# Layer norm of eight token tiles: five of them moved from ScalarE and GpSimd to VectorE

## The chip, the cores and the metric

The kernel runs on one core of a Trainium2 chip. The metric is the device time of one execution in microseconds (us). The core has five engines that run side by side: TensorE (PE in the rows; its weight loads are PEld), VectorE (DVE), ScalarE (ACT), GpSimd (POOL) and SyncE (SP), which here issues all the DMAs. Each engine works through its own instructions in order and waits on semaphores of the others.

## The reference

A decoder trunk of two layers over a stream x of 1024 tokens by 1024 channels, in float32. In each layer a projection of x feeds four token mixers; their gated outputs are merged, projected by `w_out`, and the stream is renewed by a layer norm, which is all that this change touches:

```python
def _layer_norm(x, g, b):
    mu = jnp.mean(xf, axis=-1, keepdims=True)
    var = jnp.mean(jnp.square(xf - mu), axis=-1, keepdims=True)
    y = (xf - mu) * lax.rsqrt(var + LN_EPS)
    return y * g + b
...
    out = merged @ w_out
    return _layer_norm(DEEPNORM_ALPHA * x + out, ln_g, ln_b)
```

## The kernel before

Tokens are cut into eight tiles of 128 (the partitions); a row of 1024 channels is two halves of 512. At the end of a layer the output projection runs in two passes, `col` 0 and then `col` 1, each over tiles t = 0 to 7. For one tile TensorE does 24 matmuls (8 blocks of k, three float32 products each, L245 to L247) into a PSUM tile `po`. VectorE then forms `res = ALPHA * xr + po` (L1218, `xr` is the old stream, loaded from DRAM) and its statistics (L1219). In the pass `col` 1 the row is complete, and `ln(t)` (L1160) follows at once: mean and variance (L1163, L1165), two small ScalarE activations that make a first rsqrt (L125, tiles `rs_t` and `rstd`), and one Newton step on VectorE (L1176 to L1178).

What follows depends on the tile. For t of 5, 6 and 7 (`direct`) VectorE does all of it: (res - mean) * gain for both halves (L1175) ahead of the Newton step, and (that) * rstd + bias for both halves behind it (L1181). For t of 0 to 4 VectorE makes -mean * rstd (L1184), ScalarE normalizes each half (L1186), GpSimd multiplies by the gain (L1187) and adds the bias (L1188). Gain and bias (`lnp`) are loaded once for each layer (L1208). The result `xo` is stored half by half by SyncE: to `xs` in layer 0, to `out` in layer 1.

Layer 0 goes straight over into layer 1. While the `po` matmuls of tiles 5 to 7 run, TensorE transposes tiles 0 to 3 of `xo` (`xtp`, L206); ScalarE copies each transposed block out of PSUM and rounds it (`xTr`, `xTh`, L210, L211), and GpSimd takes the remainder (`xTl`, L212). The weights `wA` of layer 1's first projection are loaded (L568), split by ScalarE (`wAh`, L576) and GpSimd (`wAl`, L577). Then `pA` begins, the first matmuls of layer 1: tokens of tiles 0 to 3 at first; the transposes of tiles 4 to 7 are placed among them. Layer 1's norm is the end of the program.

The order on every engine is set at build time by a scheduler that works from the program's order and its own cost model. Most [128, 512] tiles share a pool of 64 buffers (`U`), and [128, 1024] ones a pool of 7 (`W`).

Of the kernel before, what the change touches and what calls it, by code (L numbers as in the profile page):

```python
# [13 lines left out]
AF = mybir.ActivationFunctionType  # L14
ALU = mybir.AluOpType
# [4 lines left out]
P = 128  # L20
# [45 lines left out]
def decoder_trunk(ctx: ExitStack, tc: tile.TileContext, x, x_t, mem_t, positions, w_a, w_s, mla_q_norm, mla_w_qb,  # L66
                  mla_kv_norm, mla_w_kvb, fox_forget_bias, w_out,
                  ln_gain, ln_bias, out, dump=None):
    nc = tc.nc
    act, dve, pool, pe = nc.scalar, nc.vector, nc.gpsimd, nc.tensor  # L70
# [19 lines left out]
    def U(s, dt=F32R):  # L90
        return up.tile([P, HALF], dt, tag="U", name=nm(s))

    def W(s, w=S):
        if w <= HALF:
            return U(s, F32)[:, :w]
        return wp.tile([P, S], F32, tag="W", name=nm(s))[:, :w]
# [4 lines left out]
    def SM(s, n=1):  # L101
        return sp.tile([P, 16], F32, tag="sm", name=nm(s))[:, :n]
# [21 lines left out]
    def tfn(*args, **kw):  # L124
        i = act.activation(*args, **kw)  # L125
        if table_load[0] is not None:
            after(i, table_load[0])
        table_users.append(i)
# [501 lines left out]
    for layer in range(DEPTH):  # L630
# [252 lines left out]
        for b in range(0, NB, 2):  # L883
            t = U("ckv", F32).rearrange("p (b c) -> p b c", b=2)
# [269 lines left out]
        gb = []  # L1154
        res = {}
        nat = {}
        cs = [slice(0, HALF), slice(HALF, D)]
        dst = out[0] if last_layer else xs

        def ln(t):  # L1160
            direct = t >= 5
            mv = SM("mv", 2)
            dve.bn_aggr(mv, stats[:, t])  # L1163
            m, r, u = SM("var", 1), SM("rstd", 1), SM("rs_t", 1)
            dve.tensor_scalar(m, mv[:, 1:2], 1e-5, 1.0, ALU.add, ALU.mult)  # L1165
            tfn(u, m, AF.Ln)
            tfn(r, u, AF.Exp, scale=-0.5)
            if t < 5:
                o = W("xo")
                os = [o[:, c] for c in cs]  # L1170
            else:
                os = [U("xo", F32), U("xo", F32)]
            if direct:
                for half, c in enumerate(cs):
                    dve.scalar_tensor_tensor(os[half], res.pop((t, half)), mv[:, 0:1], gb[0][:, c], ALU.subtract, ALU.mult)  # L1175
            dve.scalar_tensor_tensor(u, r, m, r, ALU.mult, ALU.mult)  # L1176
            dve.tensor_scalar(u, u, -0.5, 1.5, ALU.mult, ALU.add)
            dve.tensor_tensor(r, r, u, ALU.mult)  # L1178
            if direct:
                for half, c in enumerate(cs):  # L1180
                    dve.scalar_tensor_tensor(os[half], os[half], r, gb[1][:, c], ALU.mult, ALU.add)  # L1181
                    nc.sync.dma_start(dst[t * P:(t + 1) * P, c], os[half])
            else:
                dve.scalar_tensor_tensor(mv[:, 1:2], mv[:, 0:1], -1.0, r, ALU.mult, ALU.mult)  # L1184
                for half, c in enumerate(cs):
                    act.activation(os[half], res.pop((t, half)), AF.Identity, scale=r, bias=mv[:, 1:2])  # L1186
                    pool.tensor_tensor(os[half], os[half], gb[0][:, c], ALU.mult)  # L1187
                    pool.tensor_tensor(os[half], os[half], gb[1][:, c], ALU.add)  # L1188
                    nc.sync.dma_start(dst[t * P:(t + 1) * P, c], os[half])
            nat[t] = [os[k // 4][:, (k % 4) * P:(k % 4) * P + P] for k in range(KT)]  # L1190

        xrs = []
# [11 lines left out]
        for col in range(2):  # L1204
            if col:
                for src in (ln_gain, ln_bias):
                    g = W("lnp")
                    nc.sync.dma_start(g, src[layer].partition_broadcast(P))  # L1208
                    gb.append(g)
            for t in range(NB):  # L1210
                fetch(4)
                if not col:
                    wo[1].append(wload_o(w_out[layer], t, 1, "wo", "U"))
                ps = PJ("po")
                toks = [tuple(m[:, (t % 4) * P:(t % 4) * P + P] for m in merged[(k, t // 4)]) for k in range(KT)]
                drain(weave(passes(ps, toks, wo[col], KT), early_x, 2, t == NB - 1))
                r = U("res", F32)
                dve.scalar_tensor_tensor(r, xrs.pop(0), ALPHA, ps, ALU.mult, ALU.add)  # L1218
                dve.bn_stats(stats[:, t, col], r)  # L1219
                res[(t, col)] = r  # L1220
                if col:
                    ln(t)
                    if t == 4 and not last_layer:
                        early_x = transpose_x(0, [nat.pop(i) for i in range(4)], True)
                    if t == 5 and not last_layer:
                        load_wA(layer + 1, 0, 4)
                        split_wA()
            wo[col] = None
# [64 lines left out]
```

## Time and profile before

| | us |
|---|---|
| median of 3 runs | 1590.06 |
| lowest and highest of them | 1589.1 and 1591.06 |
| profiled execution | 1590.93 |
| its span, first to last instruction | 1589.2 |
| busy: TensorE, VectorE, GpSimd, ScalarE | 1559.1, 1035.0, 834.8, 739.9 |

The profile is of one execution. Times in the rows count from the start of its span; 1.73 us of its time lie around the span. "Busy" is the sum of an engine's instructions. A row of a timeline that covers several like instructions (x2) gives the stretch that they take together.

### The profile page before, as it was taken

Reading aid. Unit: us, or ns where it says so; the run is one execution under the profiler, and the core shown is the slowest. Engines: PE = TensorE matmul, PEld = TensorE weight load, DVE = VectorE, ACT = ScalarE, POOL = GpSimd, SP = SyncE. Lnnn points to the kernel's source line nnn. Section 1 sums busy time; section 2 is a strip of 40 time slices with the busy share of each in tenths; the row PEclk is TensorE's granted clock in tenths of the full one; section 3 lists DMA queues with packets and bytes.
Section 4 is the critical chain, followed back from the end, with each engine's and each line's share of the span. In section 5 each row is a group of like instructions: output and inputs, shape, how many; then the busy total and the mean of one; then the engine's idle time right before and its main releaser. Section 6 shows DMA issues by size and latency. Waiting matters only on the chain.

```text
span 1589.2 us, 24849 instructions
## 1 busy us (share of the span) xinstructions
PE 1559.1 (98%) x8454; PEld 1332.1 (84%) x8454; DVE 1035.0 (65%) x2025; ACT 739.9 (47%) x1632; POOL 834.8 (53%) x991
## 2 busy tenths in 40 slices
PE   9999999999999999999999999999999999999997
PEld 8888888888888888888788888888888878888885
DVE  7456689844436788872763566898444367888638
ACT  4355656534424656440423556555344346564302
POOL 5676435765544344671836655267655433446515
PEclk9999999999999999999999999999999999999999
DMA  6311112142233211252312221122422332212413
GB/s 183 114 57 55 48 39 64 54 127 61 79 102 110 68 58 40 82 177 73 116 61 87 60 61 44 37 64 64 116 61 84 100 104 70 64 49 75 146 53 113
DMA packets 86062, 127.93 MB, mean 80 GB/s; under 512 B 13424, under 2 KB 38832, under 8 KB 85936
## 3 DMA queue, kind: packets, MB, share of 16 engines
q1 hardware_dynamic: 85936, 126.34, 25.6%
q8 instruction: 67, 1.10, 0.3%
q14 instruction: 59, 0.48, 0.1%
HBM read 89.57 MB, written 19.96 MB: 69 GB/s over the span
## 4 chain that ended last, share of the span: by engine, by line
PE 85%; DVE 7%; issue 2%; DMA 2%; POOL 2%; ACT 1%; SPq 0%; DVEq 0%; ACTq 0%; POOLq 0%
PE pj L245 12%; PE pj L246 12%; PE pj L247 12%; PE y L485 7%; PE pt L455 6%; PE sc L366 3%; PE sc L367 3%; PE pb L245 3%; PE po L245 3%; PE po L247 3%; PE po L246 3%; PE pb L247 3%; PE pb L246 3%; PE pg L245 2%; PE pg L247 1%
## 5 line engine op out<-in xcount | busy, mean ns | idle before, releaser
L245 PE MATMUL pj<-xTh,wh 128*128 128x512 f32 x832 | 331.6, 399 | 2.2 <-DVE mx L424 1.4
L247 PE MATMUL pj<-xTh,wl 128*128 128x512 f32 x832 | 326.5, 392 | 0.0
L246 PE MATMUL pj<-xTl,wh 128*128 128x512 f32 x832 | 326.0, 392 | 0.0
L157 POOL TENSOR_TENSOR wl<-wr,wh 128x512 fp32r<-128x512 f32 x168 | 229.9, 1370 | 9.8
L154 POOL TENSOR_SCALAR wh<-wr 128x512 fp32r<-128x512 f32 x168 | 116.3, 692 | 209.7 <-PE pj L246 112.9
L146 DVE TENSOR_TENSOR pl<-pt,ph 128x384 fp32r<-128x384 f32 (+1 forms) x272 | 170.4, 638 | 75.3 <-ACT ph L145 73.4
L145 ACT CAST ph<-pt 128x384 fp32r<-128x384 f32 (+1 forms) x272 | 147.0, 550 | 133.9 <-PE pt L455 127.6
L247 PEld LDWEIGHTS pj<-xTh,wl 128*128 128x128 f32 x832 | 156.4, 188 | 31.8
L245 PEld LDWEIGHTS pj<-xTh,wh 128*128 128x128 f32 x832 | 156.8, 188 | 28.8 <-DVE mx L424 1.8
L246 PEld LDWEIGHTS pj<-xTl,wh 128*128 128x128 f32 x832 | 156.8, 189 | 25.4
L436 POOL TENSOR_SCALAR p<-p,sm 128x896 f32<-128x896 f32 (+7 forms) x128 | 102.4, 801 | 144.0 <-DVE sm L435 142.4
L125 ACT ACTIVATE p<-p,mx 128x896 f32<-128x896 f32 (+7 forms) x128 | 99.5, 778 | 70.7 <-DVE mx L424 63.2
L485 PE MATMUL y<-pl,v 128*128 128x256 f32 (+1 forms) x544 | 125.5, 307 | 0.0
L125 ACT ACTIVATE mg<-pg 128x512 f32<-128x512 f32 x128 | 76.4, 597 | 88.0 <-PE pg L247 58.9
L485 PE MATMUL y<-ph,v 128*128 128x256 f32 (+1 forms) x544 | 112.6, 284 | 0.1
L455 PE MATMUL pt<-ident_r,p 128*128 128x128 f32 x704 | 110.5, 272 | 0.0
L245 PE MATMUL pb<-ybh,wh 128*128 128x512 f32 x256 | 102.9, 402 | 2.2 <-DVE opB L295 1.0
L485 PEld LDWEIGHTS y<-ph,v 128*128 128x128 f32 x544 | 93.7, 190 | 12.3 <-issue 0.9
L429 DVE TENSOR_TENSOR_SCAN kt<-kt,unseen 128x896 f32<-128x896 f32 (+3 forms) x64 | 94.5, 1489 | 10.1 <-ACT kt L125 9.8
L246 PE MATMUL pb<-ybl,wh 128*128 128x512 f32 x256 | 100.1, 391 | 0.0
L247 PE MATMUL pb<-ybh,wl 128*128 128x512 f32 x256 | 100.1, 391 | 0.0
L416 POOL TENSOR_SCALAR_AFFINE_SELECT bt<-bt 128x128 f32<-128x128 f32 x64 | 47.5, 745 | 95.0 <-ACT bt L125 91.2
(277 smaller groups left out, 3658.0 us busy)
## 6 DMA issues: line engine op xcount, KB each, us to landing
wr<-in_w_s_dram SPq DMA_DIRECT2D x168, 256.0 KB, 2.6
s<-opA SPq DMA_DIRECT2D x128, 64.0 KB, 2.0
s<-opB SPq DMA_DIRECT2D x128, 64.0 KB, 2.0
wr<-in_w_out_dram SPq DMA_DIRECT2D x32, 256.0 KB, 2.6
xr<-in_x_t_dram SPq DMA_DIRECT2D x16, 256.0 KB, 5.1
ckb<-c_d SPq DMA_DIRECT2D x8, 512.0 KB, 3.8
y_d<-y SPq DMA_DIRECT2D x16, 256.0 KB, 2.0
y<-y_d SPq DMA_DIRECT2D x16, 256.0 KB, 3.6
```

The costliest lines, as they stand in the source:

```text
L125: i = act.activation(*args, **kw)
L145: act.copy(h, src)
L146: return dve.tensor_tensor(l, src, f(h), ALU.subtract)
L154: i = pool.tensor_scalar(h, src, 1.0, 1.0, ALU.mult, ALU.mult)
L157: pool.tensor_tensor(l, src, f(h), ALU.subtract)
L245: pe.matmul(ps, ah, bh, start=k == 0, stop=False)
L246: pe.matmul(ps, ah, bl, start=False, stop=False)
L247: pe.matmul(ps, al, bh, start=False, stop=k == nk - 1)
L429: dve.tensor_tensor_scan(kt[:, ::-1], kt[:, ::-1], unseen[:, S - w:][:, ::-1], 1.0, ALU.mult, ALU.max)
L436: pool.tensor_scalar(p, p, sm, 1.0, ALU.mult, ALU.mult)
L455: pe.transpose(pt[:, c:c + P], self.p[i][:, b * P:(b + 1) * P], ident)
L485: pe.matmul(u.y[:, q0 * P:256], u.op["v"][b][:, u.head, :], src[:, s * 256 + q0 * P:s * 256 + 256], start=j == 0 and n == 0, stop=j == n_c ...
```

## The change

All eight tiles now take the path that tiles 5 to 7 took: the branch on `direct` and the one for ScalarE and GpSimd are gone, and nothing else is altered. The buffers stay as they were: a `W` tile for t of 0 to 4, two `U` tiles for the rest.

```diff
--- before.py
+++ after.py
@@ -1158,7 +1158,6 @@
         dst = out[0] if last_layer else xs
 
         def ln(t):
-            direct = t >= 5
             mv = SM("mv", 2)
             dve.bn_aggr(mv, stats[:, t])
             m, r, u = SM("var", 1), SM("rstd", 1), SM("rs_t", 1)
@@ -1170,23 +1169,14 @@
                 os = [o[:, c] for c in cs]
             else:
                 os = [U("xo", F32), U("xo", F32)]
-            if direct:
-                for half, c in enumerate(cs):
-                    dve.scalar_tensor_tensor(os[half], res.pop((t, half)), mv[:, 0:1], gb[0][:, c], ALU.subtract, ALU.mult)
+            for half, c in enumerate(cs):
+                dve.scalar_tensor_tensor(os[half], res.pop((t, half)), mv[:, 0:1], gb[0][:, c], ALU.subtract, ALU.mult)
             dve.scalar_tensor_tensor(u, r, m, r, ALU.mult, ALU.mult)
             dve.tensor_scalar(u, u, -0.5, 1.5, ALU.mult, ALU.add)
             dve.tensor_tensor(r, r, u, ALU.mult)
-            if direct:
-                for half, c in enumerate(cs):
-                    dve.scalar_tensor_tensor(os[half], os[half], r, gb[1][:, c], ALU.mult, ALU.add)
-                    nc.sync.dma_start(dst[t * P:(t + 1) * P, c], os[half])
-            else:
-                dve.scalar_tensor_tensor(mv[:, 1:2], mv[:, 0:1], -1.0, r, ALU.mult, ALU.mult)
-                for half, c in enumerate(cs):
-                    act.activation(os[half], res.pop((t, half)), AF.Identity, scale=r, bias=mv[:, 1:2])
-                    pool.tensor_tensor(os[half], os[half], gb[0][:, c], ALU.mult)
-                    pool.tensor_tensor(os[half], os[half], gb[1][:, c], ALU.add)
-                    nc.sync.dma_start(dst[t * P:(t + 1) * P, c], os[half])
+            for half, c in enumerate(cs):
+                dve.scalar_tensor_tensor(os[half], os[half], r, gb[1][:, c], ALU.mult, ALU.add)
+                nc.sync.dma_start(dst[t * P:(t + 1) * P, c], os[half])
             nat[t] = [os[k // 4][:, (k % 4) * P:(k % 4) * P + P] for k in range(KT)]
 
         xrs = []
```

The scheduler's orders change at the end of each layer alone. On ScalarE and GpSimd the five tiles' instructions drop out (10 activations and 20 tensor_tensor in each layer), and the others keep their order. Below, `mv` is mean and variance, `var`, `rs_t` and `rstd` are [128, 1] tiles, and lines behind L1160 have other numbers after the change (L1173 was L1175, L1178 was L1181, L1208 was L1218).

VectorE, layer 0, tile 0, before:

```order
L1163 BN_AGGR mv_8673<-bst_8344 128x2
L1165 TENSOR_SCALAR var_8675<-mv_8673 128x1
L1176 SCALAR_TENSOR_TENSOR rs_t_8677<-rstd_8676,var_8675 128x1
L1177 TENSOR_SCALAR rs_t_8677<-rs_t_8677 128x1
L1178 TENSOR_TENSOR rstd_8676<-rstd_8676,rs_t_8677 128x1
L1184 SCALAR_TENSOR_TENSOR mv_8673<-mv_8673,rstd_8676 128x1
L1218 SCALAR_TENSOR_TENSOR res_8721<-xr_8567,po_8696 128x512
```

and after:

```order
L1162 BN_AGGR mv_8673<-bst_8344 128x2
L1164 TENSOR_SCALAR var_8675<-mv_8673 128x1
L1173 SCALAR_TENSOR_TENSOR xo_8681<-res_8384,mv_8673,lnp_8639 128x512
L1173 SCALAR_TENSOR_TENSOR xo_8681<-res_8670,mv_8673,lnp_8639 128x512
L1174 SCALAR_TENSOR_TENSOR rs_t_8677<-rstd_8676,var_8675 128x1
L1175 TENSOR_SCALAR rs_t_8677<-rs_t_8677 128x1
L1176 TENSOR_TENSOR rstd_8676<-rstd_8676,rs_t_8677 128x1
L1178 SCALAR_TENSOR_TENSOR xo_8681<-xo_8681,rstd_8676,lnp_8641 128x512 x2
L1208 SCALAR_TENSOR_TENSOR res_8718<-xr_8567,po_8693 128x512
L1209 BN_STATS bst_8344<-res_8718 128x6
```

The two gain instructions stand between the variance and the Newton step, so that they run while ScalarE makes `rstd`; the two bias instructions stand ahead of the next tile's `res`.

VectorE, layer 0, tiles 6 (`mv_9070`) and 7 (`mv_9117`), after the change; before it the order there is the same:

```order
L1173 SCALAR_TENSOR_TENSOR xo_9078<-res_8600,mv_9070,lnp_8639 128x512
L1173 SCALAR_TENSOR_TENSOR xo_9079<-res_9067,mv_9070,lnp_8639 128x512
L1208 SCALAR_TENSOR_TENSOR res_9114<-xr_8835,po_9089 128x512
L1174 SCALAR_TENSOR_TENSOR rs_t_9074<-rstd_9073,var_9072 128x1
L1209 BN_STATS bst_8344<-res_9114 128x6
L1175 TENSOR_SCALAR rs_t_9074<-rs_t_9074 128x1
L1162 BN_AGGR mv_9117<-bst_8344 128x2
L1176 TENSOR_TENSOR rstd_9073<-rstd_9073,rs_t_9074 128x1
L1164 TENSOR_SCALAR var_9119<-mv_9117 128x1
L1178 SCALAR_TENSOR_TENSOR xo_9078<-xo_9078,rstd_9073,lnp_8641 128x512
L1178 SCALAR_TENSOR_TENSOR xo_9079<-xo_9079,rstd_9073,lnp_8641 128x512
L1173 SCALAR_TENSOR_TENSOR xo_9125<-res_8636,mv_9117,lnp_8639 128x512
```

The `res` of tile 7, which waits for TensorE's last `po`, stands ahead of the Newton step and the bias instructions of tile 6. Nothing has moved here.

SyncE, layer 0, from the loads of `xr` for the last tiles to the stores of the first five, before:

```order
L1200 DMA xr_8694<-in_x_dram 128x512
L1200 DMA xr_8745<-in_x_dram 128x512
L1189 DMA xs<-xo_8681 128x512 x2
L1200 DMA xr_8796<-in_x_dram 128x512
L1189 DMA xs<-xo_8732 128x512 x2
L1200 DMA xr_8847<-in_x_dram 128x512
L1189 DMA xs<-xo_8783 128x512 x2
L1189 DMA xs<-xo_8834 128x512 x2
L1189 DMA xs<-xo_8885 128x512 x2
L568 DMA wAr_8989<-in_w_a_dram 128x292
```

and after:

```order
L1190 DMA xr_8691<-in_x_dram 128x512
L1179 DMA xs<-xo_8681 128x512
L1190 DMA xr_8739<-in_x_dram 128x512
L1179 DMA xs<-xo_8681 128x512
L1179 DMA xs<-xo_8729 128x512
L1190 DMA xr_8787<-in_x_dram 128x512
L1179 DMA xs<-xo_8729 128x512
L1179 DMA xs<-xo_8777 128x512
L1190 DMA xr_8835<-in_x_dram 128x512
L1179 DMA xs<-xo_8777 128x512
L1179 DMA xs<-xo_8825 128x512 x2
L1179 DMA xs<-xo_8873 128x512 x2
```

The stores now wait for VectorE instead of GpSimd, and the loads of `xr` stand between the two halves of a tile's store instead of behind both. The loads of `wAr` still follow the stores of tile 4.

## Rows read from the trace of the kernel before

**Rows 1.** The page: span, then busy time, share and instructions by engine.

```profile
span 1589.2 us, 24849 instructions
...
PE 1559.1 (98%) x8454; PEld 1332.1 (84%) x8454; DVE 1035.0 (65%) x2025; ACT 739.9 (47%) x1632; POOL 834.8 (53%) x991
```

**Rows 2.** Busy time by stretch: window, length, each engine busy (instructions), clock, DMA.

```profile
735.00:780.00 45.00, 45.00 (x208) 37.25 (x207) 26.22 (x50) 11.23 (x23) 22.36 (x18) 1.00 0.30 105
780.00:820.00 40.00, 36.91 (x246) 33.31 (x245) 27.19 (x57) 17.60 (x41) 22.61 (x19) 1.00 0.25 84
```

**Rows 3.** Waits of TensorE from 780 to 820 us: total us, times, longest.

```profile
PE xtp L206 <- DVE xo L1181: 1.8, 1, 1.8
PE pA L246 <- POOL wAl L577: 0.7, 2, 0.5
PE pA L245 <- ACT xTr L210: 0.2, 1, 0.2
PE pA L245 <- DVE xTl L146: 0.2, 1, 0.2
```

**Rows 4.** VectorE, layer 1: start us, length us, instruction [idle before <-releaser].

```profile
1556.10 0.69 DVE L1218 SCALAR_TENSOR_TENSOR res<-xr,po 128x512 f32<-128x512 f32 x1 [0.45 <-PE po L247]
...
1563.97 1.30 DVE L1176 SCALAR_TENSOR_TENSOR rs_t<-rstd,var 128x1 f32<-128x1 f32 x1 [0.51 <-ACT rstd L125]
...
1569.44 2.87 DVE L1175 SCALAR_TENSOR_TENSOR xo<-res,mv,lnp 128x512 f32<-128x512 f32 x2
...
1576.09 0.68 DVE L1218 SCALAR_TENSOR_TENSOR res<-xr,po 128x512 f32<-128x512 f32 x1
...
1581.14 0.68 DVE L1218 SCALAR_TENSOR_TENSOR res<-xr,po 128x512 f32<-128x512 f32 x1
...
1582.89 1.40 DVE L1175 SCALAR_TENSOR_TENSOR xo<-res,mv,lnp 128x512 f32<-128x512 f32 x2
1584.22 0.21 DVE L1176 SCALAR_TENSOR_TENSOR rs_t<-rstd,var 128x1 f32<-128x1 f32 x1
...
1584.85 1.41 DVE L1181 SCALAR_TENSOR_TENSOR xo<-xo,rstd,lnp 128x512 f32<-128x512 f32 x2
```

**Rows 5.** TensorE's last instruction, same columns.

```profile
1577.43 0.39 PE L247 MATMUL po<-woh,mgl 128*128 128x512 f32 x1
```

**Rows 6.** GpSimd after 1520 us, the last row.

```profile
1571.72 2.99 POOL L1188 TENSOR_TENSOR xo<-xo,lnp 128x512 f32<-128x512 f32 x2
```

**Rows 7.** VectorE at the layer boundary.

```profile
778.76 2.55 DVE L1175 SCALAR_TENSOR_TENSOR xo<-res,mv,lnp 128x512 f32<-128x512 f32 x2
...
792.07 0.67 DVE L1218 SCALAR_TENSOR_TENSOR res<-xr,po 128x512 f32<-128x512 f32 x1
...
802.79 1.42 DVE L1181 SCALAR_TENSOR_TENSOR xo<-xo,rstd,lnp 128x512 f32<-128x512 f32 x2
```

**Rows 8.** TensorE at the layer boundary.

```profile
790.06 0.39 PE L247 MATMUL po<-woh,mgl 128*128 128x512 f32 x1
...
803.60 0.44 PE L206 MATMUL xtp<-ident_r,xo 128*128 128x128 f32 x2 [1.81 <-DVE xo L1181]
```

**Rows 9.** GpSimd, 725 to 822 us: the last norm rows, then the splits.

```profile
780.73 2.98 POOL L1188 TENSOR_TENSOR xo<-xo,lnp 128x512 f32<-128x512 f32 x2
783.67 5.92 POOL L212 TENSOR_TENSOR xTl<-xTr,xTh 128x512 fp32r<-128x512 f32 x4
...
804.07 1.59 POOL L577 TENSOR_TENSOR wAl<-wAr,wAh 128x292 fp32r<-128x292 f32 x2 [3.05 <-ACT wAh L576]
```

**Rows 10.** SyncE issues, 735 to 822 us.

```profile
739.18 0.33 SPq L1208 DMA_DIRECT2D lnp<-in_ln_bias_dram  x1
...
784.47 2.61 SPq L568 DMA_DIRECT2D wAr<-in_w_a_dram  x4
...
800.80 0.88 SPq L568 DMA_DIRECT2D wAr<-in_w_a_dram  x2
```

**Rows 11.** Landing of the gain and bias loads, us from issue.

```profile
DMA to landing us min/median/max: 3.6/4.3/5.4
```


## The prediction

> **What bounds the kernel now.** I began with the page: TensorE is busy for 1559.1 of 1589.2 us [rows 1]. A change outside TensorE can therefore pay in two ways only: it takes away a stretch in which TensorE stands idle, or it shortens what runs when TensorE has finished. So I looked at the two ends of a layer, where the changed code lies, by windows, waits and timelines.
>
> At the end of the program TensorE stops at 1577.43 + 0.39 = 1577.82 us [rows 5], and the span goes on to 1589.2. VectorE takes up the last tile's `res` at 1581.14 [rows 4], which is 3.32 us after its input was there. VectorE is late, and the reader can see why. At tile 3 (1556.10) `res` still waited for TensorE. In tiles 4 and 5 the short instructions swell: a [128, 1] `rs_t` took 1.30 us where tile 7's took 0.21, and the pair of gain instructions of tile 5 took 2.87 where that of tile 7 took 1.40 [rows 4]. In both cases GpSimd was multiplying and adding [128, 512] tiles beside them; its last row ends at 1574.71 [rows 6], and after that no VectorE row is swollen.
>
> At the layer boundary TensorE is full up to 780 us and idle for 40.00 - 36.91 = 3.09 us in the next 40 [rows 2]. Its waits name who was late: 1.8 us for tile 7's `xo` from VectorE, 0.7 for GpSimd's `wAl`, 0.2 for ScalarE's `xTr`, 0.2 for a later `xTl` [rows 3]. The first three trace back to the norm on GpSimd: its last norm row ends at 783.7, and only then can the splits `xTl` and `wAl` begin [rows 9]; the `wAr` loads are issued at 784.47, behind the stores of tile 4 that wait for that same row [rows 10]; and VectorE's pairs are swollen here as well (2.55 for the gain pair of tile 5) [rows 7].
>
> **The change part by part.**
>
> *Work taken off ScalarE and GpSimd.* Both engines have idle time in the two stages, so the instructions themselves buy nothing. What counts is that GpSimd then has nothing to do at the end of layer 1, and is free for its splits at the boundary.
>
> *Work put on VectorE.* Five tiles in each layer get two pairs, 1.40 + 1.41 us [rows 4], less one [128, 1] instruction. Does VectorE keep up? Undisturbed, one full tile of this kind takes 1581.14 - 1576.09 = 5.05 us from `res` to `res` (tile 6) [rows 4]. TensorE needs (1577.82 - 1556.10) / 4 = 5.43 us for a tile [rows 4, 5]. VectorE has 0.38 us to spare in each tile, so the added work lies beside TensorE and costs nothing until tile 7. Without that cover each tile would cost what it runs over. The wait for ScalarE's `rstd` lies under the gain pair, since in tile 7 `rs_t` follows the pair with no gap [rows 4].
>
> *End of the program.* With no contention and 0.38 us to spare, `res` of tile 7 starts when TensorE has finished, some hundredths after 1577.82 instead of at 1581.14. What follows is the same eight instructions and stores as now, already undisturbed. Gain: **3.3 us**. It can't be more, as TensorE's end is the floor; it is nothing if VectorE is late by as much as now.
>
> *Layer boundary.* TensorE's `po` of tile 7 ends at 790.06 + 0.39 = 790.45 [rows 8]. The order puts the `res` of tile 7 ahead of the rest of tile 6, so behind 790.5 VectorE still has the Newton step of tile 6 (1584.85 - 1584.22 = 0.63), its bias pair (1.33, from 5.05 and the other rows of tile 7: 5.05 - (1584.85 - 1581.14) = 1.34), and tile 7 up to its first finished half (1584.85 + 0.74 - 1581.14 = 4.45, with half of 1.41 as a little over 0.7): 6.4 us, so 796.9 [rows 4]. TensorE asks for that half at 803.60 - 1.81 = 801.79 now [rows 8], and 0.9 us sooner without the `wAl` and `xTr` waits: 800.9. That leaves 4 us of cover. The splits gain more still: tile 3's `xo` is finished by VectorE about one tile after its `res`, so the first transposes no longer wait for GpSimd, and GpSimd starts on `xTl` some 8 us before 783.67: tile 5's gain pair at 778.76 lies 1582.89 - 1581.14 = 1.75 behind its `res`, so VectorE will have ended tile 4 by 777.0 and tile 3 one period sooner, by 771.6 [rows 4, 7]. The `wAr` loads, behind the stores of tile 4, move as far. So the waits of 1.8, 0.7 and 0.2 go, and the last 0.2, which is a matter of the second half's transposes, stays. Gain: **2.7 us**; at most 3.09.
>
> The bound below: GpSimd still has its 16 splits here, and some will meet VectorE. Between the `res` of tile 7 and its first finished half VectorE took 802.79 + 0.74 - 792.07 = 11.46 us in this trace [rows 7], with GpSimd busy for most of it and a wait for ScalarE in it. If it took as long again, the half would be ready at 790.5 + 11.46 = 802.0, TensorE would wait 1.1 us, and the gain would be 1.6. I take the upper value: eight `xTl` at 5.92 / 4 and eight `wAl` at 1.59 / 2 are 18 us of splits [rows 9], which from 775 on would be over near 793, before most of that stretch.
>
> A rule of the Trainium skill bears on this collision (SBUF — State Buffer, section "Who interferes with whom"): a VectorE instruction with two SBUF inputs contends with a GpSimd instruction that reads SBUF, and the loser waits for the whole of the other instruction. The trace agrees as to the size: 1.30 against 0.21 us is about one GpSimd instruction longer [rows 4, 6]. By that rule the nine such instructions of the stretch could each lose one `xTl` instruction, 5.92 / 4 = 1.48 us [rows 9], which would make the half ready at 810 and turn the gain into a loss of some 7 us; by the rows the stretch took 11.46 us under just this load, and the gain of 1.6 stays.
>
> *Loads and stores.* The second of the gain and bias loads is issued at 739.18 and they land within 5.4 us [rows 10, 11], at 744.6. The first gain instruction now comes five tiles before 778.76 [rows 7], near 751: hidden. The `xr` loads stand one store half earlier in SyncE's queue than before, behind stores that VectorE now ends sooner: no cost.
>
> **Sum.** The profiled execution took 1590.93; less 3.3 and 2.7 is 1584.9. It was 0.87 slower than the median of the runs, so against that median I forecast **1584.1 us**.
>
> **The rivals.**
>
> *Only the end gains.* The boundary stays as it is, because a late `wAr` load, or splits that still collide with VectorE, puts another wait in the place of those removed. For it: 16 splits are left there, and GpSimd's `wAl` ran as late as 805.7 [rows 9]. Against it: everything that feeds them starts sooner. 1590.06 - 3.3 = 1586.8 us.
>
> *VectorE becomes the bound* (the other sign). The place is the tile period, the margin 0.38 us: if the four large instructions of a tile took over 0.1 us more each, VectorE would fall behind by a little in every tile. If a pair took 2.1 us, midway between 1.40 and 2.87 [rows 4], the period would be 6.5 us and tile 7 late by 7 x 1.1 = 7.7 us, against 3.3 now; with its own pairs 1.4 longer the end loses 5.8, and the boundary some 3: about 1599 us. Against it: without GpSimd all the pairs of tiles 6 and 7 took 1.40 or 1.41, and the buffers are of the same kinds. The Trainium skill (Perfetto Trace Analysis, "Optimizing Scalar/DVE Operations") speaks for it: where VectorE is saturated, work should rather be handed to ScalarE or GpSimd, although it adds that between VectorE and GpSimd this might not help. Here VectorE was busy for 26.22 of 45 us [rows 2] before the change, so by the trace it is not saturated.
>
> *The splits block VectorE in full.* Every two-input VectorE instruction of the boundary stretch loses one whole split: 9 x 1.48 = 13.3 us [rows 9], the half ready at 796.9 + 13.3 = 810.2 against 800.9 asked, a wait of 9.3 where 2.7 were saved: 1590.06 - 3.3 + 6.6 = 1593.4 us. Against it: 18 us of splits that start near 775 don't reach that far. The rule of the page on SBUF above is what speaks for it.
>
> *Nothing moves.* The cost sits in `res` and the statistics, not in the collisions: 1590 us. Against it are tiles 6 and 7, which ran undisturbed at 5.05.
>
> **How the numbers follow.** Both gains 0.78 (1583.7 to 1586); only the end, or one of the two in part, 0.11 (1586 to 1588.5); nothing 0.05; VectorE the bound 0.04; the splits in full 0.02. The runs shown lie 0.12% apart, so 0.2%, 3.2 us, is about what can be told from no change: faster means below 1586.9. The first case is all faster, the second about half: 0.84; no change 0.10; slower 0.06. The range goes from all of both gains (1590.06 - 3.3 - 3.1 = 1583.7) less 1.2 for the spread of the runs to the second case's middle: 1582.5 to 1587.5.
>
> **What would show it.** In the profile after, the `res` rows of layer 1 should come every 5.4 us up to tile 7, that one within 0.1 us of TensorE's end, with every pair at 1.40 and `rs_t` at 0.21. At the boundary the wait for tile 7's `xo` should be gone, the first `xTl` should start before 777 us, `wAr` be issued near 777, and TensorE's idle time between 780 and 820 us be under 0.5. Wrong would be: a `res` that drifts behind TensorE in tiles 0 to 4 of either layer, gain pairs over 1.8 us with GpSimd idle, or a new wait of `pA` for `wAl`.

## The result, and the profile after

The changed kernel takes **1581.53 us** (median of four runs, 1580.08 to 1581.85) against 1589.76 us for the kernel before (four runs, 1589.1 to 1591.06, the three of the table ahead among them). The ratio is 0.9942, with a 95% interval of 0.9929 to 0.9954. It is faster, as forecast, but by some 8.2 us where 6.0 were forecast, and it lies 1 us under the low end of the range. The profiled execution took 1581.58.

The page of the kernel after, the lines that answer to [rows 1]:

```profile
span 1579.9 us, 24800 instructions
PE 1556.5 (99%) x8454; PEld 1330.7 (84%) x8454; DVE 1036.2 (66%) x2055; ACT 724.2 (46%) x1612; POOL 783.0 (50%) x951
```

GpSimd has lost 51.8 us of work, ScalarE 15.7, and VectorE has gained 30 instructions but only 1.2 us of busy time: its norm instructions on [128, 1] operands (`rs_t`, `rstd`, `mv`) fell from 28.7 to 6.9 us in the two passes, which pays for most of the pairs that it took over. TensorE, whose work is the same, is busy for 2.6 us less and the span is 9.3 shorter; how little a busy time says here will come back below.

The end of the program first, VectorE in layer 1, columns as in [rows 4]: start, length, instruction, idle time before it.

```profile
1566.37 0.69 DVE L1208 SCALAR_TENSOR_TENSOR res<-xr,po 128x512 f32<-128x512 f32 x1 [0.30 <-PE po L247]
...
1568.14 1.41 DVE L1173 SCALAR_TENSOR_TENSOR xo<-res,mv,lnp 128x512 f32<-128x512 f32 x2
1569.46 0.22 DVE L1174 SCALAR_TENSOR_TENSOR rs_t<-rstd,var 128x1 f32<-128x1 f32 x1
...
1571.81 0.69 DVE L1208 SCALAR_TENSOR_TENSOR res<-xr,po 128x512 f32<-128x512 f32 x1 [0.30 <-PE po L247]
...
1575.53 1.41 DVE L1178 SCALAR_TENSOR_TENSOR xo<-xo,rstd,lnp 128x512 f32<-128x512 f32 x2
```

And TensorE's last instruction, as in [rows 5]:

```profile
1571.39 0.39 PE L247 MATMUL po<-woh,mgl 128*128 128x512 f32 x1
```

TensorE ends at 1571.78 and `res` of tile 7 starts at 1571.81; before, it started 3.32 us late. From tile 2 on the rows stand 5.44 us apart, each waits some 0.3 us for TensorE, and no pair and no `rs_t` is swollen. From the last `res` to the end of the span it is 8.1 us, as before. The 3.3 us of the forecast are there.

The layer boundary: busy time by stretch, as in [rows 2], and the only wait of TensorE there that is left, as in [rows 3].

```profile
780.00:820.00 40.00, 39.77 (x273) 37.37 (x272) 25.70 (x69) 12.45 (x30) 13.60 (x14) 1.00 0.16 56
```

```profile
PE pA L245 <- DVE xTl L146: 0.2, 1, 0.2
```

TensorE's idle time is 0.23 us instead of 3.09, and what remains is the wait that was forecast to remain. Its rows there, to be read against [rows 8]:

```profile
787.73 0.39 PE L247 MATMUL po<-woh,mgl 128*128 128x512 f32 x1
787.96 0.29 PE L245 MATMUL pA<-wAh,xTh 128*128 128x292 f32 x1
788.09 0.30 PE L246 MATMUL pA<-wAl,xTh 128*128 128x292 f32 x1
...
797.16 0.38 PE L206 MATMUL xtp<-ident_r,xo 128*128 128x128 f32 x2
```

From the last `po` to the transposes of tile 7 it is 797.16 - 787.73 = 9.43 us; before it was 803.60 - 790.06 = 13.54 [rows 8], with the same 64 `pA` matmuls and six transposes between the two rows. So the boundary gave 4.1 us, and not 2.7. GpSimd and SyncE, against [rows 9, 10]:

```profile
772.97 5.61 POOL L212 TENSOR_TENSOR xTl<-xTr,xTh 128x512 fp32r<-128x512 f32 x4 [51.74 <-ACT xTh L211]
778.54 4.03 POOL L577 TENSOR_TENSOR wAl<-wAr,wAh 128x292 fp32r<-128x292 f32 x4
782.53 5.93 POOL L212 TENSOR_TENSOR xTl<-xTr,xTh 128x512 fp32r<-128x512 f32 x4
791.64 2.36 POOL L577 TENSOR_TENSOR wAl<-wAr,wAh 128x292 fp32r<-128x292 f32 x2 [3.19 <-ACT wAh L576]
796.37 1.58 POOL L577 TENSOR_TENSOR wAl<-wAr,wAh 128x292 fp32r<-128x292 f32 x2 [2.37 <-ACT wAh L576]
```

```profile
773.64 2.08 SPq L568 DMA_DIRECT2D wAr<-in_w_a_dram  x4
```

The first splits start 10.7 us sooner in the span than before, the `wAr` loads are issued 10.8 sooner, and twelve of the sixteen splits are over when VectorE takes up tile 7. (Some 2.4 us of this were there already at the first `res` of the pass, so 8.3 and 8.4 belong to the change.) VectorE itself, against [rows 7]:

```profile
776.68 2.44 DVE L1173 SCALAR_TENSOR_TENSOR xo<-res,mv,lnp 128x512 f32<-128x512 f32 x2
...
780.62 2.49 DVE L1178 SCALAR_TENSOR_TENSOR xo<-xo,rstd,lnp 128x512 f32<-128x512 f32 x2
...
785.61 3.39 DVE L1173 SCALAR_TENSOR_TENSOR xo<-res,mv,lnp 128x512 f32<-128x512 f32 x2
788.93 0.68 DVE L1208 SCALAR_TENSOR_TENSOR res<-xr,po 128x512 f32<-128x512 f32 x1
...
790.68 1.41 DVE L1178 SCALAR_TENSOR_TENSOR xo<-xo,rstd,lnp 128x512 f32<-128x512 f32 x2
792.01 2.54 DVE L1173 SCALAR_TENSOR_TENSOR xo<-res,mv,lnp 128x512 f32<-128x512 f32 x2
...
795.10 1.42 DVE L1178 SCALAR_TENSOR_TENSOR xo<-xo,rstd,lnp 128x512 f32<-128x512 f32 x2
```

Here the collisions are still to be seen: pairs of 2.44 to 3.39 us beside the splits, 1.41 where GpSimd is idle. From the `res` of tile 7 to its first finished half it is 795.10 + 0.74 - 788.93 = 6.9 us, and TensorE asks 1.3 us later.

Collisions are not all that has gone here. Before, that stretch took 11.46 us, and in it VectorE stood 2.33 us waiting for ScalarE's `rstd` of tile 6 (ScalarE, then VectorE, of the kernel before):

```profile
787.58 1.35 ACT L576 CAST wAh<-wAr 128x292 fp32r<-128x292 f32 x3 [4.31 <-DMA wAr<-in_w_a_dram]
...
794.83 0.20 ACT L125 ACTIVATE rstd<-rs_t 128x1 f32<-128x1 f32 x1
```

```profile
795.07 1.02 DVE L1176 SCALAR_TENSOR_TENSOR rs_t<-rstd,var 128x1 f32<-128x1 f32 x1 [2.33 <-ACT rstd L125]
```

In ScalarE's order that `rstd` stands behind the `wAh` splits and four more pairs of `xTr` and `xTh`, and these were late because `wAr` was. After the change `rstd` is there at 786.2, and no `rs_t` of this stage waits. So about half of the 4.55 us that VectorE's stretch lost is this wait, which also goes back to GpSimd's norm, but through the stores, the `wAr` loads and ScalarE's queue.

### The profile page after: what moved, and what is told of

It reads as the page before. It is cut to its first block, busy times and chain, and to the rows that moved or that the text cites. A ratio compares the mean times of both kernels' runs of the same rounds, so it can differ in the third digit from the quotient of the medians.

```text
span 1579.9 us, 24800 instructions
## 1 busy us (share of the span) xinstructions
PE 1556.5 (99%) x8454; PEld 1330.7 (84%) x8454; DVE 1036.2 (66%) x2055; ACT 724.2 (46%) x1612; POOL 783.0 (50%) x951
## 4 chain that ended last, share of the span: by engine, by line
PE 87%; DVE 6%; POOL 2%; issue 2%; DMA 1%; ACT 1%; SPq 0%; DVEq 0%; POOLq 0%; ACTq 0%
PE pj L245 12%; PE pj L247 12%; PE pj L246 12%; PE y L485 7%; PE pt L455 6%; PE po L246 4%; PE po L245 4%; PE po L247 4%; PE sc L366 3%; PE sc L367 3%; PE pb L245 3%; PE pb L246 3%; PE pb L247 3%; PE pg L245 1%; PE pg L247 1%
## 5 line engine op out<-in xcount | busy, mean ns | idle before, releaser
L125 ACT ACTIVATE mg<-pg 128x512 f32<-128x512 f32 x128 | 76.4, 597 | 88.1 <-PE pg L247 58.9
L429 DVE TENSOR_TENSOR_SCAN kt<-kt,unseen 128x896 f32<-128x896 f32 (+3 forms) x64 | 94.5, 1489 | 10.1 <-ACT kt L125 9.8
L455 PEld LDWEIGHTS pt<-ident_r,p 128*128 128x128 f32 x704 | 84.9, 140 | 13.0
```

What stands on the lines that cost most here:

```text
L429: dve.tensor_tensor_scan(kt[:, ::-1], kt[:, ::-1], unseen[:, S - w:][:, ::-1], 1.0, ALU.mult, ALU.max)
L455: pe.transpose(pt[:, c:c + P], self.p[i][:, b * P:(b + 1) * P], ident)
```

## The experiments

The theory after the result: the gain is the sum of two places that have nothing to do with each other, 3.3 us at the end and 4.1 at the boundary, and both go back to the norm on GpSimd. At the end that is GpSimd being out of VectorE's way; at the boundary it is this together with the splits, the `wAr` loads and ScalarE's `rstd` coming sooner, and no run parts these from each other. A table at the end of this section gives both places for every profile.

### One layer at a time

Here the new form is used in layer 0 alone (every tile that isn't direct keeps the old form with ScalarE and GpSimd):

```diff
-            direct = t >= 5
+            direct = t >= 5 or not last_layer
```

> The change in layer 0 alone; layer 1 keeps the norm on ScalarE and GpSimd. Theory (three parts: the layer boundary, the end, and something ahead of both): the boundary gains about 4.1 us, since the starts of TensorE's instructions move by that much there, not the 2.7 of the prediction; the end stays late as before, so 1589.8 - 4.1 = 1585.7 us. Rival A, the idle time of the windows is the whole of the boundary gain: 1587.0. Rival B, the extra 2.2 us that the profile after gained ahead of any changed instruction belongs to the layer 0 edit: 1583.5.

Measured: 1585.31 us against 1589.88, ratio 0.9970 (0.9958 to 0.9981). The waits at the boundary are gone as in the full change, and at the end of the program VectorE is 3.5 us late. Its `res` of tile 7, and TensorE's last matmul:

```profile
1573.97 0.68 DVE L1218 SCALAR_TENSOR_TENSOR res<-xr,po 128x512 f32<-128x512 f32 x1
```

```profile
1570.11 0.39 PE L247 MATMUL po<-woh,mgl 128*128 128x512 f32 x1
```

And layer 1 alone:

```diff
-            direct = t >= 5
+            direct = t >= 5 or last_layer
```

> The change in layer 1 alone. All of layer 0 and the boundary have the same instructions in the same order as before. Theory: the end gains 3.3 us, 1586.5 us, with the res of tile 7 within 0.1 us of TensorE's end. The part ahead of the change is chance of one execution: the first res of layer 0's second pass at 746 to 749 us. Rival: that part comes with any edit (the program is shorter): 1584.2 us. Rival, VectorE becomes the bound in the tiles: 1590 or more.

Measured: 1586.92 us against the same 1589.88, ratio 0.9981 (0.9972 to 0.9990). At the boundary the waits stay, these two beside the 0.2 us that every kernel has:

```profile
PE xtp L206 <- DVE xo L1181: 1.2, 1, 1.2
PE pA L246 <- POOL wAl L577: 1.1, 2, 0.6
```

The two gains, 4.6 and 3.0 us, add up to 7.5, and each layer's interval holds what its place in the trace says. The listed waits of the boundary (2.3 us) are again less than what goes when they go. That `res` and the statistics were the cost, with nothing to gain, or that only the end could gain, is out with these two.

### Fewer tiles moved

Only tiles 3 and 4 change over; 0 to 2 keep the old form in both layers.

```diff
-            direct = t >= 5
+            direct = t >= 3
```

> Only tiles 3 and 4 are moved to VectorE in both layers; tiles 0 to 2 stay on ScalarE and GpSimd. Theory: what costs is GpSimd's work in the last tiles, since VectorE falls behind TensorE only from tile 4 on; GpSimd's last norm row ends some 12 us sooner, VectorE has caught up by tile 7 and the splits at the boundary start early. So the time is within 1 us of the full change, about 1582 us. Rival: each moved tile brings its share, two fifths of the gain: 1586.5 us.

Measured: 1583.59 us, ratio 0.9960 (0.9947 to 0.9972), between the two expectations. The boundary gains as much as with the full change (55.0 us in the table below), the end only 2.0; VectorE had not caught up by tile 7, against the theory's expectation. GpSimd's last norm row and VectorE after it, layer 1:

```profile
1553.39 2.98 POOL L1188 TENSOR_TENSOR xo<-xo,lnp 128x512 f32<-128x512 f32 x2
```

```profile
1557.76 0.68 DVE L1218 SCALAR_TENSOR_TENSOR res<-xr,po 128x512 f32<-128x512 f32 x1
...
1572.88 0.68 DVE L1218 SCALAR_TENSOR_TENSOR res<-xr,po 128x512 f32<-128x512 f32 x1
```

GpSimd is done at 1556.4, but by then VectorE is behind by 2.55 us (the rows up to tile 3 come every 5.44 us, tile 4's 7.99 later), and with a period of 5.04 it makes up 0.4 us in each tile: (1572.88 - 1557.76) / 3 = 5.04. It is still 1.4 us late when TensorE ends (1571.50). A margin of 0.4 us in a tile means that such a delay takes more than six tiles to be forgotten. At the boundary the lateness doesn't matter, since there TensorE has other work before it asks for tile 7.

### The same kernels again

The changed kernel once more, with the three above:

> The full change once more, on the same chip as the three above, to see what is chance. Theory (chance ahead of the change): the profile shows the first res of layer 0's second pass anywhere from 746 to 749 us, with one or two stretches of lower clock, and the time 1580 to 1583. Rival (the part ahead belongs to the program): again at 746.3 us with one such stretch, and 1581.5 us within 0.5.

Measured: 1581.52 us against 1589.88, ratio 0.9948 (0.9936 to 0.9960). And the kernel before, with 11 runs on another chip and one more for its profile alone:

> The kernel before once more, unchanged, to see what its own profile holds by chance. Theory (chance): a ratio of 1.000, and the first res of layer 0's second pass sooner than the 748.7 us of the first profile, between 746.5 and 748, with no stretch of lower clock near 234 us. Rival (the part ahead of the change belongs to the program): 748.7 us again, with the lower clock near 234 us, and near 1026 us once more.

Measured: 1590.15 us against 1590.15, ratio 0.9998 (0.9990 to 1.0007).

> A third profile of the kernel before. The same two expectations as for the second.

Measured: 1590.42 us. The two places of these three profiles are those of the first ones to 0.3 us (table). The expectation that what lies ahead of the change would come out shorter in the kernel before by chance was missed: its second and third profiles have the same stretch of lower clock, and the pass begins at 749.04 and 748.22 us (first profile 748.70).

### GpSimd made busy again

Is it the work that VectorE had, or GpSimd beside it? The changed kernel, with VectorE's work as it is, and in layer 1 four GpSimd products for each of tiles 0 to 4, into a scratch tile that nobody reads:

```diff
+            if last_layer and t < 5:
+                for half, c in enumerate(cs):
+                    for g in gb:
+                        pool.tensor_tensor(TMP("junk"), os[half], g[:, c], ALU.mult)
```

> The full change, and in layer 1 GpSimd is given 20 tensor_tensor of 128x512 again (products of xo with gain or bias into a scratch tile that nothing reads). No instruction of the norm waits for them. Theory (the collision of two-input instructions is what made VectorE late): the short rs_t rows swell to 1 us and more and the pairs to 2.5 to 3.5 us in tiles 1 to 5, a period of about 8 us there, res of tile 7 some 6 to 12 us behind TensorE, 1588 to 1594 us. Rival (VectorE was late because it waited for the chain over ScalarE and GpSimd, not for the port): 1581.5 us as without them.

Measured: 1591.48 us against 1590.15 for the kernel before, ratio 1.0011 (1.0002 to 1.0020). All of the gain is gone, with no instruction added to VectorE, although the boundary keeps its part (55.0 us in the table). From tile 2 on VectorE waits for nobody here; its instructions are longer. One tile of layer 1, VectorE and then GpSimd:

```profile
1544.50 0.68 DVE L1212 SCALAR_TENSOR_TENSOR res<-xr,po 128x512 f32<-128x512 f32 x1
...
1546.26 2.98 DVE L1173 SCALAR_TENSOR_TENSOR xo<-res,mv,lnp 128x512 f32<-128x512 f32 x2
1549.16 1.25 DVE L1174 SCALAR_TENSOR_TENSOR rs_t<-rstd,var 128x1 f32<-128x1 f32 x1
...
1552.15 0.68 DVE L1212 SCALAR_TENSOR_TENSOR res<-xr,po 128x512 f32<-128x512 f32 x1
```

```profile
1544.06 6.33 POOL L1183 TENSOR_TENSOR junk<-xo,lnp 128x512 f32<-128x512 f32 x4 [1.33 <-DVE xo L1178]
```

The gain pair has 1.57 us more than undisturbed and `rs_t` 1.03; the period is 7.65 us instead of 5.04, and TensorE's 5.43 is no cover for that. The span ends 56.3 us behind the first `res` of this pass, where the changed kernel takes 46.2: some 10.1 us, close to the difference of the times (1591.48 - 1581.53 = 10.0, of runs that were not taken together).

### How much more VectorE could take

The changed kernel with one more gain instruction for tiles 0 to 6 of layer 1, into a scratch tile:

```diff
+            if last_layer and t < 7:
+                dve.scalar_tensor_tensor(TMP("junk"), res[(t, 0)], mv[:, 0:1], gb[0][:, cs[0]], ALU.subtract, ALU.mult)
```

> The full change, and in layer 1 one more VectorE instruction of 0.7 us in each of tiles 0 to 6 (the gain instruction of one half once more, into a scratch tile that nothing reads). Theory (VectorE has 0.38 us to spare in a tile of 5.44): the period becomes 5.75, tile 7's res is late by 7 x 0.31 = 2.2 us, 1583.7 us. Rival (VectorE has room for more, since its instructions overlap): 1581.5 us.

Measured: 1582.36 us against 1590.15, ratio 0.9952 (0.9939 to 0.9966). The expected lateness did not come. VectorE from tile 3 to tile 4:

```profile
1549.68 0.69 DVE L1210 SCALAR_TENSOR_TENSOR res<-xr,po 128x512 f32<-128x512 f32 x1 [0.28 <-PE po L247]
1550.29 0.15 DVE L1177 TENSOR_SCALAR rs_t<-rs_t 128x1 f32<-128x1 f32 x1
1550.40 0.69 DVE L1211 BATCH_NORM_STATS2 bst<-res 128x6 f32<-128x512 f32 x1
...
1551.26 1.36 DVE L1180 SCALAR_TENSOR_TENSOR xo<-xo,rstd,lnp 128x512 f32<-128x512 f32 x2
...
1555.12 0.69 DVE L1210 SCALAR_TENSOR_TENSOR res<-xr,po 128x512 f32<-128x512 f32 x1 [0.33 <-PE po L247]
```

The first period is over TensorE's (5.71 us), but further on the order in which the instructions are written out has changed with the added one: the Newton step and the bias pair of a tile stand behind the `res` of the next, between its statistics, and the tile with the added instruction fits into 5.44 us with 0.33 to spare. The added work costs no time in the tiles. What it costs is the order: the bias pair of tile 6 now lies between the `res` of tile 7 and its end, and that stretch is 1.1 us longer (47.2 instead of 46.2). So "0.38 us to spare" was no measure of what VectorE can take.

### What is left of the difference

In the profiles the two places make 7.1 to 7.4 us; the three comparisons of the full change with the kernel before gave 7.2 to 8.4. All three profiles of the kernel before also had a stretch of some 3.4 us from about 223 us on in which the granted clock was 0.5, TensorE's level of 1.2 GHz, and the first two profiles of the changed kernel had none there. It follows a wait of TensorE in layer 0, 1.9 us that end at 222.2, far from the changed code. The changed kernel has that same wait, and its clock stayed at 1.00. Two edits that change the program and not the norm were to tell whether it belongs to one kernel: one GpSimd product, or one ScalarE copy, at the last tile, into scratch.

```diff
+            if last_layer and t == 7:
+                pool.tensor_tensor(TMP("junk"), gb[0][:, cs[0]], gb[1][:, cs[0]], ALU.mult)
```

> The kernel before with one GpSimd instruction more, a product of gain and bias into a scratch tile, in layer 1 while GpSimd is idle ahead of the first norm row. It can move nothing in the stages that the change concerns. All three profiles of before have a stretch of lower clock near 234 us of the clock records, and none of the seven edited kernels has it. Theory (that stretch hangs on the program as a whole, not on the norm): gone here, the first res of layer 0's second pass 1 to 2 us sooner, and 1588 to 1589 us against 1590. Rival (it hangs on the norm's work): still there, 1590 us.

Measured, added to the kernel before: 1590.18 us against 1588.96, ratio 1.0004 (0.9995 to 1.0013).

> The kernel before with one ScalarE copy more, of the gain into a scratch tile, in layer 1 where ScalarE is idle. The same two expectations: by the theory no lower clock near 234 us and 1588 to 1589 us; by the rival 1590 us.

Measured, `act.copy(TMP("junk"), gb[0][:, cs[0]])` in its place: 1590.43 us, ratio 1.0008 (0.9999 to 1.0016).

> The full change with the same one GpSimd instruction more. By the theory the stretch near 234 us may come back, and with it some 1.4 us: 1581.5 or 1583 us. By the rival it can't: 1581.5 us.

Measured, the GpSimd product added to the changed kernel: 1581.80 us, ratio 0.9957 (0.9944 to 0.9969). The stretch as windows show it, in the kernel before with the GpSimd product and then in the changed kernel with it (the number behind the last bracket is the granted clock, 1.00 and 0.96):

```profile
200.00:240.00 40.00, 37.35 (x215) 32.02 (x215) 35.54 (x45) 24.42 (x57) 12.71 (x15) 1.00 0.13 37
```

```profile
200.00:240.00 40.00, 37.38 (x206) 32.40 (x207) 34.03 (x44) 22.90 (x53) 11.13 (x15) 0.96 0.13 37
```

They stand the wrong way round for a property of the kernel: the slower kernel has a profile without the stretch and the faster one a profile with it. It comes in some executions and not in others. The two edits of the kernel before had no stretch near 223 us, as the theory said, but were not faster for it over all their runs (1590.18 and 1590.43 us where 1588 to 1589 were expected).

The places in all the profiles, worked out from the starts of VectorE's rows (us). "Boundary" runs from the `res` of tile 0 in the pass that ends layer 0 to an early copy of layer 1 that every kernel has (that of `kpn`); "end" from the `res` of tile 0 in the same pass of layer 1 to the end of the span; "rest" is the span less both. The last column counts the stretches of some 3.4 us at the granted clock 0.5 that lie in the rest while TensorE has work: near 223 us, near 1010 us, or both.

| kernel | boundary | end | rest | stretches in the rest |
|---|---|---|---|---|
| before, three profiles | 58.9 to 59.1 | 49.4 | 1480.4 to 1480.8 | 2 in each |
| before with the GpSimd product | 58.9 | 49.4 | 1479.7 | 1 |
| before with the ScalarE copy | 60.7 | 49.4 | 1478.7 | 1 |
| layer 1 alone | 58.9 | 46.2 | 1478.5 | 1 |
| layer 0 alone | 55.0 | 49.5 | 1477.4 | 0 |
| tiles from 3 on | 55.0 | 47.5 | 1478.5 | 1 |
| after, two profiles | 55.0 | 46.2 | 1478.7, 1479.5 | 1 in each |
| after with the GpSimd product | 55.0 | 46.1 | 1478.6 | 1 |
| after, GpSimd busy | 55.0 | 56.3 | 1476.8 | 0 |
| after, one more gain instruction | 55.0 | 47.2 | 1478.3 | 1 |

The boundary has two values, and they go with layer 0's form alone. The end is 49.4 with the old norm in layer 1 and 46.2 with the new, and takes other values only where layer 1's norm or GpSimd's load there was altered otherwise. The one exception, 60.7, has a stretch at the lower clock inside (granted clock 0.96 from 780 to 820 us, 1.00 in all the others). It begins right behind the wait for tile 7's `xo`, which the change takes away (TensorE of that profile; the granted clock is 1.00 until 801 us and 0.50 from 802 to 804):

```profile
801.31 0.60 PE L206 MATMUL xtp<-ident_r,xo 128*128 128x128 f32 x2 [1.80 <-DVE xo L1181]
```

The rest goes by the number of stretches: 1476.8 and 1477.4 us with none, 1478.3 to 1479.7 with one, 1480.4 to 1480.8 with two. With one stretch each it is 1478.7 and 1479.7 where both layers have the old norm and 1478.3 to 1479.5 where one or both have the new. So the difference in the rest between the first profiles of the two kernels, 2.0 us, is one stretch.

## Why the prediction was right, and where it was wrong

**The end of the program: right, in size too.** 3.3 us, to the floor that TensorE's end sets. The reason given, GpSimd beside VectorE, is shown by making GpSimd busy again, which brought back some 10.1 us.

**VectorE keeps up: right.** The tile period was taken as 5.05 against 5.43, and in layer 1 `res` waited some 0.3 us for TensorE in every tile from 2 on. The rival of VectorE as the bound fell twice over: without GpSimd the pairs stay at 1.41, and 0.7 us more in each tile still fitted. The argument that the buffers are of the same kinds did not hold as it stood, since tiles 0 to 4 write into `W` tiles and tiles 6 and 7 into `U` tiles, but the pairs took 1.40 to 1.42 us in both.

**The layer boundary: the right mechanism, mis-sized.** This is the term that failed: 2.7 us, "at most 3.09", came out as 4.1 (3.9 against most other profiles in the table), and with 4.1 the sum would have been 1590.06 - 3.3 - 4.1 = 1582.7, inside the range. (Of the 1.1 us that are left to the measured time, 0.3 is the lower median of the kernel before with its fourth run; 0.8 is what the two places do not hold.) The step that failed is to size the stall by TensorE's idle time and listed waits. The bound was read from TensorE's idle time and from its waits [rows 2, 3], and both are too small where matmuls follow each other closely. Rows of TensorE of the kernel before that the prediction did not use:

```profile
790.69 0.40 PE L245 MATMUL pA<-wAh,xTh 128*128 128x292 f32 x1 [0.24 <-ACT xTr L210]
790.93 0.30 PE L246 MATMUL pA<-wAl,xTh 128*128 128x292 f32 x1
791.06 0.29 PE L247 MATMUL pA<-wAh,xTl 128*128 128x292 f32 x1
...
793.24 0.30 PE L245 MATMUL pA<-wAh,xTh 128*128 128x292 f32 x1
793.64 0.40 PE L246 MATMUL pA<-wAl,xTh 128*128 128x292 f32 x1
```

A matmul of 292 columns is drawn 0.29 us long, but when nothing is late the next one starts 0.13 us after it (790.93 to 791.06); one of 512 columns is drawn 0.39 long with a start every 0.23. The rest of each length lies under the next matmul. When something is late, the first 0.16 us of the delay lie under the drawn tail and count as busy, and only what goes beyond is idle time or a wait. From 790.06 to 790.69 it is 0.63 us where 0.23 were needed: 0.40 lost, 0.24 listed. From 793.24 to 793.64 it is 0.27 lost, and there is no bracket at all. Summed from the last `po` to tile 7's transposes this is 4.11 us, where the rows' idle times say 2.75. TensorE's busy time shows the same: between these two rows it was 10.69 us before and 9.43 after for the same matmuls at the granted clock 1.00, so part of it was waiting. Layer 0 alone gained 3.0 to 6.7 us by its interval, which also leaves out 2.7.

**The cover at the boundary: right in sign, too large.** It was put at 4 us and came out as 1.3. Half of the loss is the same error (TensorE could ask for tile 7 some 1.4 us sooner than "0.9 us sooner"), the other half VectorE: the gain pair of tile 6 at 3.39 us holds up the `res` of tile 7 for 0.8 us, and tile 7's own pair took 2.54, 1.1 more than undisturbed, while the Newton step of tile 6 ran among tile 7's statistics and saved the 0.6 that were counted for it. The splits ended at 798 and not at 793. Nothing was lost by it, but 1.3 us more and this term would have shrunk.

**The splits in full: did not come, as forecast.** Twelve of the sixteen splits were over when VectorE took up tile 7. Behind the `res` of tile 7 one pair of three lost 1.13 us, about one of GpSimd's `wAl` at 2.36 / 2 = 1.18. The Trainium skill (SBUF — State Buffer, "Who interferes with whom") has the loser wait for the whole of the other instruction; for a single collision these rows agree. What it doesn't give is how many of them meet, and here that was one and not nine.

**The rest: settled in size, open in one point.** The measured 8.2 us lie 0.8 to 1.1 above the two places. The intervals of the three comparisons with the changed code (7.3 to 11.3, 6.4 to 10.2 and 4.9 to 8.9 us, worked out from the ratios) hold 7.4 in every case, so nothing more need be there. The "rest" of the profiles scatters by 4 us, and it goes by the stretches of lower clock, which the prediction left out: some 1.7 us each. Whether the change makes them rarer stays open. In the five profiles with the old norm in both layers there were two, two, two, one and two, the one at the boundary counted in; in the eight others none or one. The stretch at the boundary stood behind a wait that the change removes, but the others stand behind waits that every kernel has, and no run was made to tell.

## What to carry to other kernels

Size a stall of TensorE from the starts of its matmuls, counted from a row before the stall to one after it, and not from idle time or listed waits: here these showed 2.75 of 4.11 us. Look for GpSimd beside VectorE wherever VectorE's pairs or its [128, 1] instructions swell; to give VectorE more instructions and GpSimd none can make a stage faster, if VectorE's undisturbed period is under that of the engine that sets the pace. A margin of some tenths in a tile is only good for as many tiles as come after the last collision: three tiles at 0.4 us did not make up for 2.55.

## What the runs showed of the hardware that was not expected

Both sides pay for a collision. In the busy kernel four GpSimd products beside VectorE took 6.33 us where before two took 2.54 in tiles 1 to 3, as the row below shows (kernel before, GpSimd, layer 1), and VectorE lost 2.6 us in a tile.

```profile
1559.16 2.54 POOL L1188 TENSOR_TENSOR xo<-xo,lnp 128x512 f32<-128x512 f32 x2
```

Not every instruction of VectorE swells beside GpSimd. Of the [128, 1] ones, those that read two tiles of SBUF did, and those that read one did not; here in the kernel before, both layers (instructions | busy us, mean ns | idle before), where the first line's mean is 249 after the change and the second's 153:

```profile
L1176 DVE SCALAR_TENSOR_TENSOR rs_t<-rstd,var 128x1 f32<-128x1 f32 x16 | 11.2, 699 | 9.4 <-ACT rstd L125 9.4
L1177 DVE TENSOR_SCALAR rs_t<-rs_t 128x1 f32<-128x1 f32 x16 | 2.4, 152 | 0.5
```

`res`, which reads one operand from SBUF and one from PSUM, stayed at 0.67 to 0.69 us in every row shown.

In one kernel VectorE's short instructions cost less where an independent one stands between them and what they depend on; that this is the reason was not tested by itself. In the kernel with one more gain instruction the step of 0.15 us starts at 1550.29, before the 0.69 us of `res` at 1549.68 are over, and a whole tile took 5.44 - 0.33 = 5.1 us with 0.74 us of work more than a tile of the changed kernel, which took 5.44 - 0.30 = 5.1.

The granted clock falls to TensorE's lower level (1.2 GHz) for some 3.4 us in some executions and not in others, behind waits of TensorE of 1.8 to 1.9 us. Such a wait does not always bring it: every profile has one near 222 and one near 1010 us, but the first profile of the kernel before has a stretch behind both and that of the changed one only behind the second. At half the clock 3.4 us hold the work of 1.7, so one such stretch can cost up to 1.7 us, an estimate from its length. The table agrees: 60.7 against 58.9 us at the boundary, and some 1.7 us in the rest for each. That is more than the 1.4 by which the boundary term was off.
